# High and low parts of x^T side by side: one 512-column product with the high weights, and the halves added on eviction

## The chip, the cores and the metric

The kernel runs on one core of one Trainium2 chip. The metric is device time in microseconds from start to end of the program, the median of several runs. TensorE (PE) multiplies, VectorE (DVE) and ScalarE (ACT) read its results out of PSUM and prepare its operands, GpSimd (POOL) does a few small powers, and SyncE (SP) issues the DMAs that bring the weights.

## The reference

Four transformer blocks and then a fifth of another kind work on x of 256 tokens by 1024 features, all in fp32. The parts that the change touches, cut down:

```python
def conv_glu_ffn(x, w_up, conv_w, conv_b, w_down):      # four times, D_FF = 2816
    h = causal_depthwise_conv(x @ w_up, conv_w, conv_b) # kernel of 3 tokens
    g, u = jnp.split(h, 2, axis=-1)
    return (jax.nn.silu(g) * u) @ w_down
...
q = rope(q, cos, sin, dk); k = rope(k, cos, sin, dk)    # retention: 4 heads of 256, q and k from u @ w_in
...
f = jnp.square(jax.nn.relu(v2 @ w_up[i])) @ w_down[i]   # the fifth block's MLP, 4096 wide
```

Between them lie attention of several kinds, a linear recurrence, cross attention to a memory, and norms.

## The kernel before

An fp32 product is made of three products in TensorE's faster fp32r format: each operand is split into a high part (ScalarE, `split`, L200) and the low rest (VectorE, L201), and high x high, high x low and low x high are added up in PSUM. The activations stand transposed in two tiles, `xTh` and `xTl`, of 128 partitions x 8 chunks k x 256 tokens. `mm_T` (L218 to L225) makes the three products of one chunk for a result of 128 features x 256 tokens: the weights are the stationary operand, 256 token columns stream past them, and every product loads its weights anew (wh for L222 and L223, wl for L224). `proj_T` runs over the eight chunks, which is called a block of up products here. `mm_nat` (L214 to L216) is the other orientation, with 512 weight columns streaming.

Weights come in 512 KB pieces: a DMA into one of 5 `raw` tiles, then `split` into one of 9 pairs of `wh` and `wl` tiles of 1024 columns. A queue of each engine runs in program order, which a scheduler has fixed when the kernel was built; semaphores make one engine wait for another.

A feed-forward block (`ffn`, phases b0f to b3f) goes over 11 pairs p of 256 features. `up(p)` makes four blocks: for the gate half and the value half (b), two blocks (j), of which j = 0 lies in a PSUM bank of tag `sc` and j = 1 in one of tag `tr`, two banks of each tag. `conv` reads each block three times: ScalarE scales the last tap and adds the bias (L520), VectorE adds the two older taps (L522). `glu` then takes a tanh on ScalarE (L528), two steps on VectorE (L529, L530), and splits the result into `q` (high, ScalarE) and `pT` (low, VectorE). `down` of an earlier pair follows each `up`: 24 products of 512 columns into four banks that gather the block's result. The pairs 0 and 1 take their up products in the other orientation and are transposed (`nat_up`), which makes the start of a block rich in VectorE's work; the last pairs' down products come together in `down_end`. From pair 4 on, `up(p)` and a `down` make one period.

`mlp` does the same for 16 pairs without convolution: one bank holds both halves of a pair, VectorE takes maximum with 0 (L1443) and square (L1444). `ret_proj` projects q and k of a retention head into one bank of tag `sc` and rotates them on VectorE straight out of PSUM. The gates of the recurrence, the latent attention and the memory's keys use `proj_T` too.

Of the kernel before, what the change touches and what calls it, by code (L numbers as in the profile page):

```python
# [12 lines left out]
F32 = mybir.dt.float32  # L13
F32R = mybir.dt.float32r
I32 = mybir.dt.int32
AF = mybir.ActivationFunctionType
ALU = mybir.AluOpType
AX = mybir.AxisListType.X

P = 128  # L20
D = 1024
T = 256
NT = 2
KD = D // P
# [139 lines left out]
class Net:  # L164
# [66 lines left out]
    def proj_T(self, ps, cols, c0, Th, Tl):  # L231
        if Th is self.xTh:
            self.need()
        for k in range(cols.K):
            self.mm_T(ps, cols.get(k), slice(c0, c0 + P), Th[:, k, :], Tl[:, k, :], k == 0, k == cols.K - 1)

    def defer(self, cols, t, f):

        self.pend.append((self.work + cols, t, f))
# [36 lines left out]
            self.T_split(src, hi, lo)  # L276

    def new_xT(self):
        self.xTh = self.xp.tile([P, KD, T], F32R, tag="xTh", name=self.nm("xTh"))
        self.xTl = self.xp.tile([P, KD, T], F32R, tag="xTl", name=self.nm("xTl"))  # L280

    def new_oT(self):
        return (self.op.tile([P, KD, T], F32R, tag="oTh", name=self.nm("oTh")),
# [226 lines left out]
    def ffn(self, i, cc, pool):  # L510
        nc, I = self.nc, self.I
# [4 lines left out]
        def conv(ps, b, p):  # L516
            hc = self.s("e", [2, T])
            for j in range(2):
                f = b * NFT + 2 * p + j
                nc.scalar.activation(hc[:, j], ps[j], AF.Identity, bias=cc[:, 3, f : f + 1], scale=cc[:, 2, f : f + 1])  # L520
                for s in (1, 2):
                    nc.vector.scalar_tensor_tensor(hc[:, j, s:], ps[j][:, : T - s], cc[:, 2 - s, f : f + 1],  # L522
                                                   hc[:, j, s:], ALU.mult, ALU.add)
            return hc
# [10 lines left out]
        def up(p):  # L535
            gu = []
            for b in range(2):
                w = self.cols(W, b * DFF + p * 256, 256)
                pss = []
                for j in range(2):  # L540
                    ps = self.ps(("sc", "tr")[j], (T,))
                    self.proj_T(ps, w, j * P, self.xTh, self.xTl)
                    pss.append(ps)
                gu.append(conv(pss, b, p))
            return glu(*gu)

        def nat_up(nat, p):
# [31 lines left out]
        nat = self.op.tile([P, 2, 2, 512], F32, tag="oTh", name=self.nm("nat"))  # L579
        nat = [self.nat_chunk(ws, t, nat[:, t]) for t in range(NT)]  # L580
        hl[2] = up(2)
        hl[0] = nat_up(nat, 0)
        hl[3] = up(3)
        hl[1] = nat_up(nat, 1)
        tail = self.ln_tail(i, 2)
# [294 lines left out]
    def mla(self, j, mp):  # L880
        nc, I = self.nc, self.I
# [28 lines left out]
        sc = 192.0 ** -0.5  # L910
# [69 lines left out]
        down(1)  # L980
        norm(0)
        norm(1)
        v = self.xp.tile([P, 2, D], F32, tag="xTh", name=self.nm("v"))
        for hf in range(2):
            wq, wkv, qrT = w = weights(hf)
            for t in range(NT):
# [290 lines left out]
    def ret_proj(self, out, h):  # L1277
        nc = self.nc
        W = self.I["w_in_2"][0]
        for c0, tag in ((0, "C"), (1024, "D")):  # L1280
            w = self.cols(W, c0 + h * 256, 256)
            ps = self.ps("sc", (2, T))
            for j in range(2):
                self.proj_T(ps[:, j], w, j * P, self.xTh, self.xTl)
            a, b = self.b2(tag, [2, T]), self.s("e", [2, T])
            C = self.cos[:, None, :T].to_broadcast([P, 2, T])
            S = self.sin[:, :T]
            nc.vector.tensor_mul(a, ps, C)
            nc.vector.tensor_mul(b[:, 0], ps[:, 1], S)
            nc.vector.tensor_mul(b[:, 1], ps[:, 0], S)  # L1290
            nc.vector.tensor_sub(a[:, 0], a[:, 0], b[:, 0])
            nc.vector.tensor_add(a[:, 1], a[:, 1], b[:, 1])
            out.append(a)
            yield
        w = self.cols(W, 2048 + h * 512, 512)
        v, sg = self.b2("A", [2, 512]), self.b2("B", [2, 512])
        out += [v, sg]
        for t in range(NT):
            ps = self.ps("sc")
            self.proj_nat(ps, self.xTh, self.xTl, t, w)  # L1300
            nc.scalar.activation(v[:, t], ps, AF.Copy)
            yield
        w = self.cols(W, 4096 + h * 512, 512)
        for t in range(NT):
            ps = self.ps("sc")
            self.proj_nat(ps, self.xTh, self.xTl, t, w)
            a = sg[:, t]
            nc.scalar.activation(a, ps, AF.Tanh, scale=0.5)
            nc.vector.scalar_tensor_tensor(a, a, 1.0, ps, ALU.add, ALU.mult)
            yield  # L1310
# [120 lines left out]
    def mlp(self):  # L1431
        nc, I = self.nc, self.I
# [3 lines left out]

        def up(p):
            w = self.cols(W, p * 256, 256)
            ps = self.ps(("sc", "tr")[p % 2], (2, T))
            for j in range(2):  # L1440
                self.proj_T(ps[:, j], w, j * P, self.xTh, self.xTl)
            r, r2 = self.s("e", [2, T]), self.s("p", [2, T])
            nc.vector.tensor_scalar_max(r, ps, 0.0)  # L1443
            nc.vector.tensor_mul(r2, r, r)  # L1444
            hi, lo = self.s("q", [2, T], F32R), self.s("pT", [2, T], F32R)
            self.split(r2, hi, lo)
            return hi, lo
# [42 lines left out]
        for p in range(5, NPR):  # L1490
            hl[p] = up(p)
            flush(p - 1)
            if p == 7:
                e = self.ple_e()
# [126 lines left out]
```

## Time and profile before

| | |
|---|---|
| runs | 2077.45, 2081.17, 2081.6 us; median 2081.17 |
| profiled execution | 2078.6 us, span 2076.8 |
| TensorE busy | 2040.2 us, 98% of the span, 12213 products and as many weight loads |
| VectorE, ScalarE busy | 1539.4 us (74%), 1196.2 us (58%) |
| TensorE's clock | 2.4 GHz, mean granted share 0.997 |
| DMA | 359.83 MB, mean 173 GB/s |

Busy time of TensorE is modelled from its pipelined products, so starts of successive products tell more than durations. An engine's idle time matters only where TensorE ends up waiting for it.

### The profile page before, as it was taken

The numbers are of one execution on the slowest core, as the hardware profiler recorded it, in microseconds if no ns is written. First come the engines' busy times: TensorE is split into PE (matmuls) and PEld (weight loads), VectorE is DVE, ScalarE is ACT, GpSimd is POOL, SyncE is SP. The second block draws the span as 40 slices with busy tenths as digits, with TensorE's granted clock in tenths as the row PEclk, the third lists the DMA queues.
The fourth block names the chain that finished last, engine by engine and source line by source line (L and its number), as shares of the span: only waits on it lengthen the run. The fifth ranks groups of instructions, "written<-read, shape, count | busy, mean of one in ns | idle before, by whom it ended". The sixth has DMA issues, their size and how long they took to land.

```text
span 2076.8 us, 33251 instructions
## 1 busy us (share of the span) xinstructions
PE 2040.2 (98%) x12213; PEld 1784.0 (86%) x12213; DVE 1539.4 (74%) x2972; ACT 1196.2 (58%) x2408; POOL 39.8 (2%) x54
## 2 busy tenths in 40 slices
PE   7999999999999999999999999999999999999998
PEld 6878999887899988889997789998898888788896
DVE  7766887899697777779778778878666665676666
ACT  5844655596476546556656556555675444555544
POOL 0000000000000000000000000000000000000000
PEclk9999999999999999999999999999999999999999
DMA  7353666447466543565654436664545556566562
GB/s 269 127 187 115 210 209 188 147 134 249 137 202 194 171 161 111 183 198 179 190 156 160 144 124 213 215 187 120 164 123 192 166 176 203 166 199 206 188 188 76
DMA packets 236659, 359.83 MB, mean 173 GB/s; under 512 B 13904, under 2 KB 157392, under 8 KB 236496
## 3 DMA queue, kind: packets, MB, share of 16 engines
q1 hardware_dynamic: 236496, 357.71, 53.8%
q8 instruction: 96, 1.57, 0.3%
q14 instruction: 67, 0.55, 0.1%
HBM read 356.60 MB, written 1.05 MB: 172 GB/s over the span
## 4 chain that ended last, share of the span: by engine, by line
PE 52%; DVE 3%; ACT 2%; DMA 1%; issue 1%; POOL 0%; SPq 0%; POOLq 0%; DVEq 0%; ACTq 0%
PE mlp.acc L214 1%; PE mlp.acc L215 1%; PE mlp.acc L216 1%; PE b3f.tr L222 1%; PE b3f.sc L222 1%; PE b2f.tr L224 1%; PE b2f.tr L223 1%; PE b2f.tr L222 1%; PE b3f.tr L223 1%; PE b3f.tr L224 1%; PE b2f.sc L224 1%; PE b3f.sc L224 1%; PE b3f.sc L223 1%; PE b2f.sc L223 1%; PE b2f.sc L222 1%; PE b2f.acc L214 1%
## 5 line engine op out<-in xcount | busy, mean ns | idle before, releaser
L201 DVE TENSOR_TENSOR mlp.wl<-mlp.raw,mlp.wh 128x512 fp32r<-128x512 f32 x132 | 86.0, 687 | 56.1 <-ACT mlp.wh L200 55.2
L200 ACT ACTIVATE mlp.wh<-mlp.raw 128x512 fp32r<-128x512 f32 x132 | 75.8, 624 | 59.3 <-issue 23.5
L200 ACT ACTIVATE b0f.wh<-b0f.raw 128x512 fp32r<-128x512 f32 x132 | 77.4, 624 | 33.4 <-PE b0f.tr L223 11.9
L200 ACT ACTIVATE b1f.wh<-b1f.raw 128x512 fp32r<-128x512 f32 x132 | 77.4, 624 | 32.8 <-PE b1f.tr L223 11.9
L200 ACT ACTIVATE b2f.wh<-b2f.raw 128x512 fp32r<-128x512 f32 x132 | 77.5, 624 | 32.2 <-PE b2f.tr L223 11.9
L200 ACT ACTIVATE b3f.wh<-b3f.raw 128x512 fp32r<-128x512 f32 x132 | 77.3, 624 | 28.8 <-PE b3f.tr L223 10.3
L201 DVE TENSOR_TENSOR b0f.wl<-b0f.raw,b0f.wh 128x512 fp32r<-128x512 f32 x132 | 85.7, 686 | 9.2 <-ACT b0f.wh L200 7.2
L201 DVE TENSOR_TENSOR b1f.wl<-b1f.raw,b1f.wh 128x512 fp32r<-128x512 f32 x132 | 85.7, 686 | 8.4 <-ACT b1f.wh L200 6.4
L201 DVE TENSOR_TENSOR b2f.wl<-b2f.raw,b2f.wh 128x512 fp32r<-128x512 f32 x132 | 85.6, 686 | 8.0 <-ACT b2f.wh L200 6.1
L201 DVE TENSOR_TENSOR b3f.wl<-b3f.raw,b3f.wh 128x512 fp32r<-128x512 f32 x132 | 85.7, 686 | 7.4 <-ACT b3f.wh L200 5.4
L222 PE MATMUL b3f.tr<-b3xo.xTh,b3f.wh 128*128 128x256 f32 x144 | 40.8, 283 | 0.0
L222 PE MATMUL b0f.sc<-b0xo.xTh,b0f.wh 128*128 128x256 f32 x144 | 40.8, 283 | 0.0
L222 PE MATMUL b1f.sc<-b1xo.xTh,b1f.wh 128*128 128x256 f32 x144 | 40.8, 283 | 0.0
L222 PE MATMUL b2f.sc<-b2xo.xTh,b2f.wh 128*128 128x256 f32 x144 | 40.8, 283 | 0.0
L222 PE MATMUL b3f.sc<-b3xo.xTh,b3f.wh 128*128 128x256 f32 x144 | 40.8, 283 | 0.0
L224 PE MATMUL b0f.tr<-b0xo.xTh,b0f.wl 128*128 128x256 f32 x144 | 40.8, 283 | 0.0
L224 PE MATMUL b1f.tr<-b1xo.xTh,b1f.wl 128*128 128x256 f32 x144 | 40.8, 283 | 0.0
L224 PE MATMUL b2f.tr<-b2xo.xTh,b2f.wl 128*128 128x256 f32 x144 | 40.8, 283 | 0.0
L222 PE MATMUL b0f.tr<-b0xo.xTh,b0f.wh 128*128 128x256 f32 x144 | 40.8, 283 | 0.0
L223 PE MATMUL b0f.tr<-b0xo.xTl,b0f.wh 128*128 128x256 f32 x144 | 40.8, 283 | 0.0
L222 PE MATMUL b1f.tr<-b1xo.xTh,b1f.wh 128*128 128x256 f32 x144 | 40.8, 283 | 0.0
L223 PE MATMUL b1f.tr<-b1xo.xTl,b1f.wh 128*128 128x256 f32 x144 | 40.8, 283 | 0.0
(1636 smaller groups left out, 7630.2 us busy)
## 6 DMA issues: line engine op xcount, KB each, us to landing
b0f.raw<-in_f_w_up_dram SPq DMA_DIRECT2D x44, 512.0 KB
b1f.raw<-in_f_w_up_dram SPq DMA_DIRECT2D x44, 512.0 KB
b2f.raw<-in_f_w_up_dram SPq DMA_DIRECT2D x44, 512.0 KB
b3f.raw<-in_f_w_up_dram SPq DMA_DIRECT2D x44, 512.0 KB
mlp.raw<-in_w_up_dram SPq DMA_DIRECT2D x32, 512.0 KB
mlp.raw<-in_w_down_dram SPq DMA_DIRECT2D x32, 512.0 KB
b0f.raw<-in_f_w_down_dram SPq DMA_DIRECT2D x22, 512.0 KB
b1f.raw<-in_f_w_down_dram SPq DMA_DIRECT2D x22, 512.0 KB
```

The source lines that it names most:

```text
L200: self.nc.scalar.activation(hi, src, AF.Copy)
L201: self.nc.vector.tensor_sub(lo, src, hi.bitcast(F32))
L214: mm(ps, Th[:, k, tok(t)], wh, start=start, stop=False)
L215: mm(ps, Th[:, k, tok(t)], wl, start=False, stop=False)
L216: mm(ps, Tl[:, k, tok(t)], wh, start=False, stop=stop)
L222: mm(ps, wh[:, cs], rh, start=start, stop=False)
L223: mm(ps, wh[:, cs], rl, start=False, stop=False)
L224: mm(ps, wl[:, cs], rh, start=False, stop=stop)
```

## The change

`xTh` and `xTl` become the two halves of one tile `xT` of 8 chunks x 2 x 256 columns. A new function `proj_x` takes the place of `proj_T` in the feed-forward blocks, in `mlp` and for q and k of the retention; the other callers of `proj_T` keep it. Per chunk, the high weights meet both halves in one product of 512 columns that fills a whole bank: the first half of the bank gathers wh x xTh, the second wh x xTl. The low weights meet xTh in a product of 256 columns that is added into the second half. At the end ScalarE copies the second half to SBUF, and VectorE adds the first half to it. The convolution, the rotation and the square then read from SBUF instead of PSUM; in `mlp` maximum and square become one instruction, and a half of a pair takes a bank of its own. The tile `v` of the latent attention, which shared the place of `xTh`, is now declared as large as `xT`.

```diff
@@ -234,6 +234,29 @@
         for k in range(cols.K):
             self.mm_T(ps, cols.get(k), slice(c0, c0 + P), Th[:, k, :], Tl[:, k, :], k == 0, k == cols.K - 1)
 
+    def proj_x(self, dst, tag, w, c0):
+
+
+        self.need()
+        ps = self.ps(tag, (2, T))
+        mm = self.nc.tensor.matmul
+        cs = slice(c0, c0 + P)
+        for k in range(w.K):
+            wh, wl = w.get(k)
+
+            def high():
+                mm(ps.rearrange("p a n -> p (a n)"), wh[:, cs], self.xT[:, k].rearrange("p a n -> p (a n)"),
+                   start=k == 0, stop=k == w.K - 1)
+
+            def low():
+                mm(ps[:, 1], wl[:, cs], self.xTh[:, k], start=False, stop=False)
+
+            for f in (high, low) if k == 0 else (low, high):
+                f()
+            self.tick(T)
+        self.nc.scalar.activation(dst, ps[:, 1], AF.Copy)
+        self.nc.vector.tensor_add(dst, ps[:, 0], dst)
+
     def defer(self, cols, t, f):
 
         self.pend.append((self.work + cols, t, f))
@@ -276,8 +299,8 @@
             self.T_split(src, hi, lo)
 
     def new_xT(self):
-        self.xTh = self.xp.tile([P, KD, T], F32R, tag="xTh", name=self.nm("xTh"))
-        self.xTl = self.xp.tile([P, KD, T], F32R, tag="xTl", name=self.nm("xTl"))
+        self.xT = self.xp.tile([P, KD, 2, T], F32R, tag="xT", name=self.nm("xT"))
+        self.xTh, self.xTl = self.xT[:, :, 0], self.xT[:, :, 1]
 
     def new_oT(self):
         return (self.op.tile([P, KD, T], F32R, tag="oTh", name=self.nm("oTh")),
@@ -536,12 +559,10 @@
             gu = []
             for b in range(2):
                 w = self.cols(W, b * DFF + p * 256, 256)
-                pss = []
+                s = self.s("p", [2, T])
                 for j in range(2):
-                    ps = self.ps(("sc", "tr")[j], (T,))
-                    self.proj_T(ps, w, j * P, self.xTh, self.xTl)
-                    pss.append(ps)
-                gu.append(conv(pss, b, p))
+                    self.proj_x(s[:, j], ("sc", "tr")[j], w, j * P)
+                gu.append(conv([s[:, 0], s[:, 1]], b, p))
             return glu(*gu)
 
         def nat_up(nat, p):
@@ -980,7 +1001,7 @@
         down(1)
         norm(0)
         norm(1)
-        v = self.xp.tile([P, 2, D], F32, tag="xTh", name=self.nm("v"))
+        v = self.xp.tile([P, 2, 2, D], F32, tag="xT", name=self.nm("v"))[:, 0]
         for hf in range(2):
             wq, wkv, qrT = w = weights(hf)
             for t in range(NT):
@@ -1279,10 +1300,9 @@
         W = self.I["w_in_2"][0]
         for c0, tag in ((0, "C"), (1024, "D")):
             w = self.cols(W, c0 + h * 256, 256)
-            ps = self.ps("sc", (2, T))
+            a, b, ps = self.b2(tag, [2, T]), self.s("e", [2, T]), self.s("e", [2, T])
             for j in range(2):
-                self.proj_T(ps[:, j], w, j * P, self.xTh, self.xTl)
-            a, b = self.b2(tag, [2, T]), self.s("e", [2, T])
+                self.proj_x(ps[:, j], "sc", w, j * P)
             C = self.cos[:, None, :T].to_broadcast([P, 2, T])
             S = self.sin[:, :T]
             nc.vector.tensor_mul(a, ps, C)
@@ -1436,12 +1456,10 @@
 
         def up(p):
             w = self.cols(W, p * 256, 256)
-            ps = self.ps(("sc", "tr")[p % 2], (2, T))
+            r, r2 = self.s("e", [2, T]), self.s("p", [2, T])
             for j in range(2):
-                self.proj_T(ps[:, j], w, j * P, self.xTh, self.xTl)
-            r, r2 = self.s("e", [2, T]), self.s("p", [2, T])
-            nc.vector.tensor_scalar_max(r, ps, 0.0)
-            nc.vector.tensor_mul(r2, r, r)
+                self.proj_x(r[:, j], ("sc", "tr")[j], w, j * P)
+            nc.vector.scalar_tensor_tensor(r2, r, 0.0, r, ALU.max, ALU.mult)
             hi, lo = self.s("q", [2, T], F32R), self.s("pT", [2, T], F32R)
             self.split(r2, hi, lo)
             return hi, lo
```

TensorE's queue at the first block of up products in feed-forward block 1 (tile names carry a number; `b1xo.xTh`, `b1xo.xTl` and `b1xo.xT` hold the transposed activations), before:

```order
L222 MATMUL b1f.sc_5962<-b1xo.xTh_5680,b1f.wh_5965 128x256
L223 MATMUL b1f.sc_5962<-b1xo.xTl_5681,b1f.wh_5965 128x256
L224 MATMUL b1f.sc_5962<-b1xo.xTh_5680,b1f.wl_5966 128x256
L222 MATMUL b1f.sc_5962<-b1xo.xTh_5680,b1f.wh_5965 128x256
L223 MATMUL b1f.sc_5962<-b1xo.xTl_5681,b1f.wh_5965 128x256
L224 MATMUL b1f.sc_5962<-b1xo.xTh_5680,b1f.wl_5966 128x256
L222 MATMUL b1f.sc_5962<-b1xo.xTh_5680,b1f.wh_5965 128x256
```

The same place of TensorE's queue now:

```order
L248 MATMUL b1f.sc_5759<-b1xo.xT_5477,b1f.wh_5762 128x512
L252 MATMUL b1f.sc_5759<-b1xo.xT_5477,b1f.wl_5763 128x256 x2
L248 MATMUL b1f.sc_5759<-b1xo.xT_5477,b1f.wh_5762 128x512
L252 MATMUL b1f.sc_5759<-b1xo.xT_5477,b1f.wl_5763 128x256
L248 MATMUL b1f.sc_5759<-b1xo.xT_5477,b1f.wh_5762 128x512
L252 MATMUL b1f.sc_5759<-b1xo.xT_5477,b1f.wl_5763 128x256
```

Two products of each chunk's three are one, and from the second chunk on the low weights come first.

VectorE's queue in a steady period of the same block, from the first read of a pair's first block on (`e` is the convolution's tile, `p` the tanh's), before:

```order
L522 SCALAR_TENSOR_TENSOR b1f.e_6876<-b1f.sc_6810,b1x.cols_5208,b1f.e_6876 128x255
L522 SCALAR_TENSOR_TENSOR b1f.e_6876<-b1f.sc_6810,b1x.cols_5208,b1f.e_6876 128x254
L201 TENSOR_TENSOR b1f.wl_7101<-b1f.raw_7098,b1f.wh_7100 128x512 x2
L201 TENSOR_TENSOR b1f.wl_7161<-b1f.raw_7158,b1f.wh_7160 128x512
L522 SCALAR_TENSOR_TENSOR b1f.e_6876<-b1f.tr_6851,b1x.cols_5208,b1f.e_6876 128x255
L201 TENSOR_TENSOR b1f.wl_7161<-b1f.raw_7158,b1f.wh_7160 128x512
L522 SCALAR_TENSOR_TENSOR b1f.e_6876<-b1f.tr_6851,b1x.cols_5208,b1f.e_6876 128x254
L529 SCALAR_TENSOR_TENSOR b1f.e_6876<-b1f.p_6956,b1f.e_6876 128x512
L522 SCALAR_TENSOR_TENSOR b1f.e_6949<-b1f.sc_6883,b1x.cols_5208,b1f.e_6949 128x255
L522 SCALAR_TENSOR_TENSOR b1f.e_6949<-b1f.sc_6883,b1x.cols_5208,b1f.e_6949 128x254
```

The same place of VectorE's queue in a steady period now (`p` is also the tile of the added halves):

```order
L258 TENSOR_TENSOR b1f.p_6518<-b1f.sc_6519,b1f.p_6518 128x256
L545 SCALAR_TENSOR_TENSOR b1f.e_6573<-b1f.p_6518,b1x.cols_5005,b1f.e_6573 128x255
L545 SCALAR_TENSOR_TENSOR b1f.e_6573<-b1f.p_6518,b1x.cols_5005,b1f.e_6573 128x254
L201 TENSOR_TENSOR b1f.wl_6773<-b1f.raw_6770,b1f.wh_6772 128x512 x2
L258 TENSOR_TENSOR b1f.p_6518<-b1f.tr_6554,b1f.p_6518 128x256
L201 TENSOR_TENSOR b1f.wl_6825<-b1f.raw_6822,b1f.wh_6824 128x512 x2
L545 SCALAR_TENSOR_TENSOR b1f.e_6573<-b1f.p_6518,b1x.cols_5005,b1f.e_6573 128x255
L545 SCALAR_TENSOR_TENSOR b1f.e_6573<-b1f.p_6518,b1x.cols_5005,b1f.e_6573 128x254
L258 TENSOR_TENSOR b1f.p_6580<-b1f.sc_6581,b1f.p_6580 128x256
L552 SCALAR_TENSOR_TENSOR b1f.e_6573<-b1f.p_6642,b1f.e_6573 128x512
```

An add (L258) now stands ahead of each block's two convolution steps, and weight splits move by a place or two; their number in a period stays 12.

VectorE's queue at the start of that block, up to the low part `pT` of pair 0, before:

```order
L522 SCALAR_TENSOR_TENSOR b1f.e_6214<-b1f.sc_6148,b1x.cols_5208,b1f.e_6214 128x255
L529 SCALAR_TENSOR_TENSOR b1f.e_6121<-b1f.p_6140,b1f.e_6121 128x512
L522 SCALAR_TENSOR_TENSOR b1f.e_6133<-b1f.tr_6128,b1x.cols_5208,b1f.e_6133 128x255
L522 SCALAR_TENSOR_TENSOR b1f.e_6214<-b1f.sc_6148,b1x.cols_5208,b1f.e_6214 128x254
L522 SCALAR_TENSOR_TENSOR b1f.e_6133<-b1f.tr_6128,b1x.cols_5208,b1f.e_6133 128x254
L522 SCALAR_TENSOR_TENSOR b1f.e_6214<-b1f.tr_6189,b1x.cols_5208,b1f.e_6214 128x255
L530 SCALAR_TENSOR_TENSOR b1f.e_6133<-b1f.e_6121,b1f.e_6133 128x512
L522 SCALAR_TENSOR_TENSOR b1f.e_6214<-b1f.tr_6189,b1x.cols_5208,b1f.e_6214 128x254
L201 TENSOR_TENSOR b1f.wl_6426<-b1f.raw_6423,b1f.wh_6425 128x512
L201 TENSOR_TENSOR b1f.pT_6145<-b1f.e_6133,b1f.q_6144 128x512
```

The same place at the start of the block now, up to the same low part:

```order
L545 SCALAR_TENSOR_TENSOR b1f.e_5907<-b1f.tr_5902,b1x.cols_5005,b1f.e_5907 128x254
L552 SCALAR_TENSOR_TENSOR b1f.e_5895<-b1f.p_5914,b1f.e_5895 128x512
L258 TENSOR_TENSOR b1f.p_5922<-b1f.sc_5923,b1f.p_5922 128x256
L553 SCALAR_TENSOR_TENSOR b1f.e_5907<-b1f.e_5895,b1f.e_5907 128x512
L258 TENSOR_TENSOR b1f.p_5922<-b1f.tr_5958,b1f.p_5922 128x256
L545 SCALAR_TENSOR_TENSOR b1f.e_5977<-b1f.p_5922,b1x.cols_5005,b1f.e_5977 128x255
L258 TENSOR_TENSOR b1f.p_5984<-b1f.sc_5985,b1f.p_5984 128x256
L201 TENSOR_TENSOR b1f.pT_5919<-b1f.e_5907,b1f.q_5918 128x512
```

The adds of pair 3's first three blocks stand in front of this low part now, and three of the four convolution steps of pair 3 that stood there come behind it.

## Rows read from the trace of the kernel before

**Rows 1.** Page, busy time and instructions of each engine; TensorE's granted clock by slice.
```profile
PE 2040.2 (98%) x12213; PEld 1784.0 (86%) x12213; DVE 1539.4 (74%) x2972; ACT 1196.2 (58%) x2408; POOL 39.8 (2%) x54
...
PEclk9999999999999999999999999999999999999999
```

**Rows 2.** TensorE's longest wait: total us, times, longest us.
```profile
PE b0swa.acc L214 <- ACT start.xTh L200: 5.5, 2, 4.9
```

**Rows 3.** Groups by line, TensorE: count, then busy us, mean ns and idle us before.
```profile
L222 PE MATMUL b1f.sc<-b1xo.xTh,b1f.wh 128*128 128x256 f32 x144 | 40.8, 283 | 0.0
L222 PE MATMUL mlp.sc<-wo.xTh,mlp.wh 128*128 128x256 f32 x96 | 27.1, 283 | 0.0
L222 PE MATMUL rp1.sc<-b3f.xTh,rp1.wh 128*128 128x256 f32 x32 | 9.1, 285 | 0.0
```

**Rows 4.** Timeline, TensorE in feed-forward block 1: start us, duration us, line, operation.
```profile
699.97 0.28 PE L224 MATMUL b1f.tr<-b1xo.xTh,b1f.wl 128*128 128x256 f32 x1
707.17 0.28 PE L224 MATMUL b1f.tr<-b1xo.xTh,b1f.wl 128*128 128x256 f32 x1
707.29 0.40 PE L214 MATMUL b1f.acc<-b1f.wh,b1f.q 128*128 128x512 f32 x1
712.08 0.39 PE L214 MATMUL b1f.tq<-b1f.wh,b1f.q 128*128 128x512 f32 x1
```

**Rows 5.** Windows, two periods: us; PE, PEld, DVE, ACT, POOL busy; clock; DMA.
```profile
645.66:662.64 16.98, 16.98 (x122) 16.02 (x121) 13.13 (x23) 10.11 (x20) 0.00 (x0) 1.00 0.59 186
662.64:679.62 16.98, 16.98 (x122) 16.02 (x121) 13.13 (x23) 10.11 (x20) 0.00 (x0) 1.00 0.59 186
```

**Rows 6.** Groups by line, VectorE, 600 to 800 us: operands of 128x256.
```profile
L622 DVE TENSOR_TENSOR b2mla.e<-b2mla.acc,ropeC 128x256 f32<-128x256 f32 x4 | 1.7, 416 | 0.0
L626 DVE TENSOR_TENSOR b2mla.e<-b2mla.e,b2mla.e 128x256 f32<-128x256 f32 x4 | 1.7, 418 | 0.0
```

**Rows 7.** Groups by line, ScalarE, 600 to 800 us: operands of 128x256.
```profile
L200 ACT ACTIVATE b2mla.oTh<-b2mla.po 128x256 fp32r<-128x256 f32 x3 | 1.2, 384 | 4.2 <-PE b2mla.po L972 4.2
L200 ACT ACTIVATE b2mla.wh<-b2mla.raw 128x256 fp32r<-128x256 f32 x6 | 2.4, 406 | 0.0
```

**Rows 8.** Groups by line, ScalarE, three periods: idle us before them, releaser.
```profile
L200 ACT ACTIVATE b1f.wh<-b1f.raw 128x512 fp32r<-128x512 f32 x38 | 22.5, 625 | 6.1 <-PE b1f.tr L223 5.2 <-PE b1f.tq L216 0.8
L200 ACT ACTIVATE b1f.q<-b1f.e 128x512 fp32r<-128x512 f32 x3 | 1.9, 632 | 5.9 <-DVE b1f.e L530 5.9
L528 ACT ACTIVATE b1f.p<-b1f.e 128x512 f32<-128x512 f32 x3 | 1.9, 632 | 3.7 <-DVE b1f.e L522 3.7
```

**Rows 9.** Groups by line, VectorE, the same three periods.
```profile
L201 DVE TENSOR_TENSOR b1f.wl<-b1f.raw,b1f.wh 128x512 fp32r<-128x512 f32 x36 | 23.7, 687 | 2.2 <-ACT b1f.wh L200 1.2
L522 DVE SCALAR_TENSOR_TENSOR b1f.e<-b1f.sc,b1x.cols,b1f.e 128x255 f32<-128x255 f32 x6 | 2.9, 480 | 4.5 <-ACT b1f.e L520 4.5
L529 DVE SCALAR_TENSOR_TENSOR b1f.e<-b1f.p,b1f.e 128x512 f32<-128x512 f32 x3 | 2.1, 693 | 2.3 <-ACT b1f.p L528 2.3
L201 DVE TENSOR_TENSOR b1f.pT<-b1f.e,b1f.q 128x512 fp32r<-128x512 f32 x3 | 2.1, 693 | 2.3 <-ACT b1f.q L200 2.3
```

**Rows 10.** Start of feed-forward block 1: window as rows 5; then VectorE's and TensorE's timeline.
```profile
578.85:597.60 18.75, 18.75 (x159) 18.75 (x158) 17.05 (x35) 14.29 (x27) 0.00 (x0) 1.00 0.46 145
...
578.85 1.00 DVE L522 SCALAR_TENSOR_TENSOR b1f.e<-b1f.sc,b1x.cols,b1f.e 128x255 f32<-128x255 f32 x2 [0.59 <-ACT b1f.e L520]
596.91 0.69 DVE L201 TENSOR_TENSOR b1f.pT<-b1f.e,b1f.q 128x512 fp32r<-128x512 f32 x1
...
600.41 0.40 PE L216 MATMUL b1f.acc<-b1f.wh,b1f.pT 128*128 128x512 f32 x1
```

**Rows 11.** End of feed-forward block 1: timeline of VectorE, then TensorE.
```profile
728.25 0.69 DVE L201 TENSOR_TENSOR b1f.pT<-b1f.e,b1f.q 128x512 fp32r<-128x512 f32 x1 [0.76 <-ACT b1f.q L200]
...
730.19 0.39 PE L216 MATMUL b1f.acc<-b1f.wh,b1f.pT 128*128 128x512 f32 x1
```

**Rows 12.** Groups by line, VectorE, 1830 to 2000 us.
```profile
L1443 DVE TENSOR_SCALAR mlp.e<-mlp.sc 128x512 f32<-128x512 f32 x4 | 2.7, 684 | 0.0
```

## Prediction

> **What bounds the kernel now.** I read the page's busy times first: of a span of 2076.8 us TensorE is busy 2040.2, at the full clock in every slice [rows 1], so all its waits together are 36.6 us. The longest of them, by the view of who waits for whom, stands at the kernel's first stage [rows 2]. The groups by line then show that the products this change touches wait for nothing: idle 0.0 us before them in the feed-forward blocks, in `mlp` and in the retention projections [rows 3]. So time is won or lost in two ways only: by how long TensorE's stream of products is, and by whether the other engines still keep ahead of it.
>
> The timeline gives the stream's price. From one 256-column product at 699.97 us to another at 707.17 lie 60 steps: 0.1200 us each. From 707.29 to 712.08 lie 21 steps of 512 columns: 0.2281 us each [rows 4]. (The durations in such rows, 0.28 and 0.40, overlap; the starts count.) Twice the columns cost less than twice the time: each product carries about 0.012 us that doesn't depend on its width. The boundary between the kinds shows no price of its own: the first wide product starts 0.12 us after the last narrow one [rows 4].
>
> **The change, part by part.** *Removed on TensorE.* Per weight chunk k, three products of 256 columns (0.360 us) become one of 512 and one of 256. A feed-forward block in its steady state repeats a period of 16.98 us, all of it TensorE's [rows 5]: 4 blocks of 24 narrow products and 24 wide ones of the down projection. 96 x 0.120 = 11.52 leaves 5.46 for 24 wide ones, 0.2275 each, boundaries included. So a merge saves 0.240 - 0.2275 = 0.0125 us by the period, 0.0119 by the steps. The merged products are counted by the L222 groups: 8 groups of 144 in four feed-forward blocks, 2 of 96 in `mlp`, 4 of 32 in retention [rows 3]: 1152 + 192 + 128 = 1472. That is 17.5 to 18.4 us; I take 18.2. 1472 weight loads go too; they lay beside the products and give nothing more.
>
> The Trainium skill speaks against this size: in "TensorE: Matmul & The Clock Gate", section Back-to-back issue gap, the gap of a warm product is its columns over 2.4 plus 2.5 ns, which makes 109 and 216 ns where the rows have 120 and 228. By that rule a merge would save 2.5 ns and the whole change 3.7 us.
>
> *Added on eviction.* One ScalarE copy and one VectorE add of 128x256 for each of 184 blocks (36 in each feed-forward block, 24 in `mlp`, 16 in retention). The trace has no such add of the kernel's own, but rope's products of the same shape took 416 ns from PSUM and 418 from SBUF [rows 6], so I take 0.418, and where a source moves from PSUM to SBUF (the convolution, the rotation) VectorE gains and loses nothing. A ScalarE eviction of 128x256 took 384 ns from PSUM, a conversion of that size from SBUF 406 [rows 7]: 0.384 for the copy, and some 0.02 more for each convolution start that now reads SBUF.
>
> *Feed-forward, steady state.* VectorE 13.13 + 4 x 0.418 = 14.80 us and ScalarE 10.11 + 4 x 0.41 = 11.75 us [rows 5], in a period that shrinks by 32 x 0.0125 to 16.58. Both fit, if their waits give way: VectorE has 3.85 us of idle per period and may keep 1.78. Over three periods its idle is 4.5 us before the convolution's first step (which hangs on TensorE ending a block), 2.2 before weight splits, and 2.3 + 2.3 behind ScalarE's tanh and high part [rows 9]. Only the last two hang on VectorE's own chain: 1.53 us a period, under 1.78 by a quarter of a microsecond. ScalarE's conversions wait for TensorE to free a weight buffer [rows 8], nine of which hold one and a half periods (6 buffers are used up in one), so a late VectorE eats that lead before TensorE stands. I price the steady state at no loss.
>
> *Feed-forward, start.* Here VectorE is full: of the 18.75 us from 578.85 to the end of the low part at 597.60 it is busy 17.05, and TensorE reads that low part at 600.41 [rows 10]. The order ahead of it gains 7 adds and loses 3 convolution steps that now come later, 7 x 0.418 - 3 x 0.48 = 1.5 us; TensorE, two groups of up products nearer, arrives 0.8 us earlier. 2.8 - 1.5 - 0.8 leaves 0.5 us, more if the 1.7 us of idle fill. If nothing fills and an add in front of a full queue waits on TensorE as well, TensorE stands for about 1 us. Four such starts: 0 to 4 us, I take 0.6.
>
> *Feed-forward, end.* The last pair's low part is done at 728.94 and read at 730.19 [rows 11]: 1.25 us of room. Copy and add lengthen the chain from the last block by 0.384 + 0.418 and two handovers, about 0.9. Covered, by 0.3 us; without the cover up to 0.9 each at four ends. I take 0.4 in all.
>
> *`mlp` and retention.* In `mlp` maximum and square (0.684 us for the first [rows 12]) become one instruction, so VectorE pays 2 x 0.418 - 0.68 = 0.15 us per pair; the result is used one pair of up products later, over 5 us. Each half takes a bank of its own now, two of each tag, so a bank comes back after two pairs instead of four, still over 10 us. In retention two banks serve four halves: a bank's eviction has the other half's 2.78 us, against 0.8 for copy and add and up to two queued weight splits of 0.69 [rows 9]. The queued conversion or split in front of the copy is the work that could be late; I price it at nothing, 1 us at most over four heads.
>
> *Waits added.* ScalarE's convolution start now waits for VectorE's add, and behind it stand weight conversions; who waits for these is TensorE, one and a half periods later. Taking wl before wh at k > 0 asks for the low weights 0.24 us earlier, which that lead covers. DMAs stay the same in number and order.
>
> Sum: -18.2 + 0.6 + 0.4 = -17.2 us on the profiled execution's 2078.6 (span 2076.8, 1.8 around it): 2061.4. That execution lies 2.6 us under the median of the runs, 2081.17; from the median it would be 2063.9. I predict between them, 2062.5.
>
> **The rivals.** *A, VectorE's lag at the start of the feed-forward blocks reaches TensorE.* For it: the full stretch [rows 10], in which eight adds (3.3 us) fall. Against: PSUM is read out by two short steps instead of three, so banks come free earlier. If each of four blocks loses 2 us, with the ends 0.9: 11.6 of 18.2 come back, 2072; at half of it 2067.
>
> *B, the width-independent 0.012 us is mostly not saved*, because a product pays again when its neighbour has another width, which mixed runs now have all along. The rows show two pure runs and one boundary at 0.12, which speaks against it. With 0.0025 us left per merge: 1472 x 0.0025 = 3.7 us, 2075 to 2077. That is also the result of the skill's gap rule named above; the trace's 0.1200 and 0.2281 don't agree with it.
>
> *C, slower: ScalarE and VectorE hand each other the blocks and can't fill their idle.* The place is the steady period. Each add waits for a copy, each convolution start for an add, in queues that run in order. If VectorE's idle stays above 2.18 us a period (16.98 - 14.80), the period is longer than now; if all 3.85 stays it is 18.65, or 1.67 more in 28 periods, 47 us, less 4 us saved elsewhere: 2122. Against it: of the 3.85 only 1.53 is tied to VectorE's chain [rows 9].
>
> *D, more than the sum*, where TensorE's remaining 36.6 us of waits shrink as well; nothing in the profile asks for it: under 2058.
>
> **How the numbers follow.** The forecast (14 to 20 us off) 0.70, A 0.14, B 0.06, C 0.06, D 0.04. The range reaches from 2058, all of 18.4 and a low run, to 2072, rival A in full: it leaves out B, C and D, 0.16. A measurement of this kernel tells about 0.2%, 4.2 us, from no change: the forecast, A and D are faster by more than that, 0.88; B is within it, 0.06; C slower, 0.06.
>
> **What would show it.** In the changed profile 10741 products, 1472 of the merged form about 0.228 us apart from the next and 1472 narrow ones at 0.120; a period of 16.58 us with VectorE near 14.8 and ScalarE near 11.8 busy, and no idle before the up products. Adds near 0.42, copies near 0.38. A: idle before the first down products of each block, behind its low part. B: a pair of starts 0.357 apart instead of 0.347. C: periods over 16.98 with TensorE idle behind weight splits. I'm wrong if TensorE's total of waits grows by more than 5 us or if the pair isn't at 0.347.

## The result and the profile after

The changed kernel took 2067.65 us (median of 4 runs, 2066.98 to 2068.26), the kernel before 2080.75 (4 runs, 2077.45 to 2081.6): ratio 0.9934, 95% interval 0.9922 to 0.9946. Two later series of the changed kernel, 5 runs each, gave 2067.89 and 2069.42. 2062.5 was forecast, with 2058 to 2072 as the range: the time lies inside, 5 us above the centre. The profiled execution took 2067.32 us, 11.3 less than that of before, where the sum was 17.2.

The page's busy times of the engines:

```profile
PE 2027.3 (98%) x10741; PEld 1704.8 (83%) x10741; DVE 1587.2 (77%) x3144; ACT 1247.6 (60%) x2592; POOL 39.8 (2%) x54
```

Two of TensorE's waits, from the view of who waits for whom (total us, times, longest):

```profile
PE b0swa.acc L214 <- ACT start.xT L200: 5.1, 2, 4.5
...
PE b3f.sc L248 <- DVE b3f.e L545: 1.0, 1, 1.0
```

Against [rows 1]: 1472 products fewer, TensorE 12.9 us less busy, and its waits 2065.5 - 2027.3 = 38.2 us instead of 36.6. [rows 2] has come down by 0.4, and of the waits in the stages that the change touches one of 1.0 us is new (and one of 0.3 in `mlp`). So the other engines kept ahead, and what is missing in these stages is missing in the stream itself. Three steady periods of feed-forward block 1 in the windows (columns as in rows 5), with their sum, answer to [rows 5]:

```profile
643.38:660.00 16.62, 16.62 (x89) 14.25 (x88) 15.23 (x30) 10.89 (x22) 0.00 (x0) 1.00 0.67 212
660.00:676.63 16.63, 16.63 (x89) 14.25 (x88) 14.77 (x29) 11.73 (x24) 0.00 (x0) 1.00 0.66 198
676.63:693.26 16.63, 16.63 (x90) 14.25 (x88) 14.16 (x28) 11.10 (x23) 0.00 (x0) 1.00 0.63 192
sum 49.88, PE 49.88 PEld 42.75 DVE 44.16 ACT 33.71 POOL 0.00; mean PE 16.63 PEld 14.25 DVE 14.72 ACT 11.24 POOL 0.00
```

16.63 us, all of it TensorE's, where 16.98 stood and 16.58 was forecast: 0.35 us for 32 merges, 0.0109 each. TensorE's timeline inside the second of these periods shows why it isn't 0.0125:

```profile
660.82 0.40 PE L248 MATMUL b1f.sc<-b1xo.xT,b1f.wh 128*128 128x512 f32 x1
...
662.59 0.40 PE L248 MATMUL b1f.sc<-b1xo.xT,b1f.wh 128*128 128x512 f32 x1
662.82 0.40 PE L248 MATMUL b1f.tr<-b1xo.xT,b1f.wh 128*128 128x512 f32 x1
...
663.63 0.39 PE L248 MATMUL b1f.tr<-b1xo.xT,b1f.wh 128*128 128x512 f32 x1
...
665.36 0.40 PE L248 MATMUL b1f.tr<-b1xo.xT,b1f.wh 128*128 128x512 f32 x1
665.59 0.39 PE L248 MATMUL b1f.sc<-b1xo.xT,b1f.wh 128*128 128x512 f32 x1
```

From 660.82 to 662.59 lie five pairs of a wide and a narrow product: 0.354 us each. In the next block, from 663.63 to 665.36, five pairs take 0.346 each. The first block runs from 660.00 to 662.82, the second to 665.59: 2.82 and 2.77. Long and short blocks take turns like this from pair 4 of every feed-forward block on, and in `mlp`. Both are the same instructions on the same shapes at the full clock; I call the two patterns of starts the long and the short one. The groups by line show the same split as mean durations (count, then busy us, mean ns and idle us before), against [rows 3]:

```profile
L248 PE MATMUL b1f.sc<-b1xo.xT,b1f.wh 128*128 128x512 f32 x144 | 52.4, 398 | 0.0
...
L248 PE MATMUL b1f.tr<-b1xo.xT,b1f.wh 128*128 128x512 f32 x144 | 51.7, 394 | 0.0
```

The second missing piece is the clock. Windows over the stretches of the profiled execution in which TensorE's granted clock (the last but two of the columns) was at half, 1.2 GHz, ahead of the kernel's tail:

```profile
52.61:56.02 3.41, 3.41 (x14) 2.92 (x14) 2.60 (x5) 3.21 (x12) 0.00 (x0) 0.50 0.05 15
465.62:469.03 3.41, 3.41 (x9) 2.66 (x9) 3.41 (x6) 2.82 (x6) 0.00 (x0) 0.50 0.60 196
1435.01:1438.42 3.41, 3.40 (x13) 3.31 (x14) 2.06 (x7) 1.69 (x3) 0.00 (x0) 0.50 0.39 115
1462.31:1465.72 3.41, 3.41 (x15) 3.30 (x14) 1.16 (x5) 2.80 (x8) 0.00 (x0) 0.50 0.40 115
```

Four, and in the execution of before two (at 1212.7 and 1468.7 us). Each costs at most half its length, 1.7 us. The profiled difference then adds up: 1472 x 0.0109 = 16.0 saved, less 1.6 of waits and up to 3.4 of half clock, leaves 11.0 or more, where 11.3 was measured.

The stages themselves say it more directly. The windows over the four feed-forward blocks, the stages with q and k of the four retention heads, and `mlp`, each from its first product to the next stage's, have these sums, before and now:

```profile
sum 1018.49, PE 1017.83 PEld 932.80 DVE 776.37 ACT 589.20 POOL 10.78; mean PE 127.23 PEld 116.60 DVE 97.05 ACT 73.65 POOL 1.35
...
sum 1003.45, PE 1001.73 PEld 850.92 DVE 823.08 ACT 637.95 POOL 10.81; mean PE 125.22 PEld 106.36 DVE 102.89 ACT 79.74 POOL 1.35
```

The stages of the change are 15.0 us shorter, and the rest of the span, where all the stretches at half clock lie, is 3.7 us longer.

### The profile page after: what moved, and what is told of

Read it like the earlier page. It is cut to its first block, busy times and chain, and to the rows that moved or that the text cites. A ratio compares the mean times of both kernels' runs of the same rounds, so it can differ in the third digit from the quotient of the medians.

```text
span 2065.5 us, 30420 instructions
## 1 busy us (share of the span) xinstructions
PE 2027.3 (98%) x10741; PEld 1704.8 (83%) x10741; DVE 1587.2 (77%) x3144; ACT 1247.6 (60%) x2592; POOL 39.8 (2%) x54
## 4 chain that ended last, share of the span: by engine, by line
PE 51%; DVE 3%; ACT 2%; issue 1%; DMA 1%; POOL 0%; SPq 0%; POOLq 0%; DVEq 0%; ACTq 0%
PE b2f.sc L248 2%; PE b2f.tr L248 2%; PE b3f.sc L248 1%; PE b3f.tr L248 1%; PE mlp.sc L248 1%; PE mlp.tr L248 1%; PE mlp.acc L214 1%; PE mlp.acc L216 1%; PE mlp.acc L215 1%; PE b2f.acc L216 1%; PE b2f.sc L252 1%; PE b3f.acc L214 1%; PE b2f.acc L214 1%; PE b3f.acc L216 1%; PE b3f.acc L215 1%; PE b2f.acc L215 1%
## 5 line engine op out<-in xcount | busy, mean ns | idle before, releaser
L248 PE MATMUL b3f.sc<-b3xo.xT,b3f.wh 128*128 128x512 f32 x144 | 52.4, 398 | 1.0 <-DVE b3f.e L545 1.0
L248 PE MATMUL b1f.sc<-b1xo.xT,b1f.wh 128*128 128x512 f32 x144 | 52.4, 398 | 0.0
L248 PE MATMUL b2f.sc<-b2xo.xT,b2f.wh 128*128 128x512 f32 x144 | 52.4, 398 | 0.0
L248 PE MATMUL b0f.sc<-b0xo.xT,b0f.wh 128*128 128x512 f32 x144 | 52.4, 398 | 0.0
L248 PE MATMUL b2f.tr<-b2xo.xT,b2f.wh 128*128 128x512 f32 x144 | 51.8, 395 | 0.0
L248 PE MATMUL b0f.tr<-b0xo.xT,b0f.wh 128*128 128x512 f32 x144 | 51.7, 394 | 0.0
L248 PE MATMUL b1f.tr<-b1xo.xT,b1f.wh 128*128 128x512 f32 x144 | 51.7, 394 | 0.0
L248 PE MATMUL b3f.tr<-b3xo.xT,b3f.wh 128*128 128x512 f32 x144 | 51.7, 394 | 0.0
L545 DVE SCALAR_TENSOR_TENSOR b1f.e<-b1f.p,b1x.cols,b1f.e 128x255 f32<-128x255 f32 (+1 forms) x72 | 34.2, 479 | 6.8 <-ACT b1f.e L543 6.3
L545 DVE SCALAR_TENSOR_TENSOR b2f.e<-b2f.p,b2x.cols,b2f.e 128x255 f32<-128x255 f32 (+1 forms) x72 | 34.2, 478 | 6.8 <-ACT b2f.e L543 6.4
```

What stands on the lines that cost most here:

```text
L248: mm(ps.rearrange("p a n -> p (a n)"), wh[:, cs], self.xT[:, k].rearrange("p a n -> p (a n)"), start=k == 0, stop=k == w.K - 1)
```

## The experiments

**The merge undone, the eviction kept.** At the first chunk the wide product stays (it opens both halves of the bank at once), at the other seven it is split again.

```diff
-            for f in (high, low) if k == 0 else (low, high):
+            def narrow():
+                mm(ps[:, 0], wh[:, cs], self.xTh[:, k], start=False, stop=False)
+                mm(ps[:, 1], wh[:, cs], self.xTl[:, k], start=False, stop=k == w.K - 1)
+
+            for f in (high, low) if k == 0 else (low, narrow):
```

> The merge alone is undone: at seven of eight chunks three products of 256 columns again; banks of two halves, copy and add stay. If the eviction is nearly free and the products give the time, 1288 products come back at 0.360 - 0.349 = 0.0106 us, 13.7 us: 2081 us, and blocks of up products last 2.87 us. If the eviction costs several microseconds, this kernel must lie above the kernel before by that cost less the 2 us of the merges that stay: 2080.75 + 4 - 2 = 2083 us or more, with TensorE's waits longer than the 38.2 us now.

2082.47 us (11 runs) against 2081.26 of before (16 runs), ratio 1.0005 [0.9996, 1.0014]. A steady period in the windows:

```profile
666.29:683.23 16.94, 16.94 (x117) 15.81 (x116) 14.32 (x28) 11.24 (x23) 0.00 (x0) 1.00 0.63 192
```

16.94 where 28 unmerged products at 0.0109 ask for 16.63 + 0.31: the gain sits in the merge alone, and copy and add cost nothing in the steady state. With the 2.0 us (184 x 0.0109) of merges that stay, the median puts the eviction at 2082.47 + 2.0 - 2081.26 = 3.2 us for the whole kernel, give or take 2 by the interval, which decides between neither of the two expectations; TensorE's waits are 39.4 us here. By the sum over the stages (1020.5 us) it is 4.0. But 2.6 of that are waits for banks at the starts of the feed-forward blocks (0.32 in three, 1.59 in the last) where the changed kernel has one of 1.0, so this kernel shows more than the eviction costs there.

**The eviction undone, the merge kept** (feed-forward blocks; cut: the switch in `proj_x` that returns the bank's first half and leaves out copy and add).

```diff
-                s = self.s("p", [2, T])
-                for j in range(2):
-                    self.proj_x(s[:, j], ("sc", "tr")[j], w, j * P)
-                gu.append(conv([s[:, 0], s[:, 1]], b, p))
+                gu.append(conv([self.proj_x(None, ("sc", "tr")[j], w, j * P, False) for j in range(2)], b, p))
```

> In the feed-forward blocks copy and add are left out, and the convolution reads the first half of the bank; the second half (both small terms of the product) is left out of the result there. The products stay. If the eviction is hidden but for the one wait of 1.0 us in the last feed-forward block and some tenths at the others, 1 to 2 us less: 2066. If the eviction is what the missing 4 us of the forecast went to, 2063.5 or less, by waits that vanish at the starts of the blocks.

2065.48 us (5 runs, 2059.95 to 2067.79), ratio 0.9918 [0.9906, 0.993]: 2.2 under the changed kernel's first median. The period is 16.63 here too; the wait of 1.0 us in the last feed-forward block is down to 0.15, and the span differs by 1.8 us, of which one stretch at half clock less (three instead of four) explains up to 1.7. The sum over the stages, which no such stretch touches, is 1002.0 instead of 1003.45: 1.5 us, 0.9 of it in the last feed-forward block. So the eviction in these blocks costs one to two microseconds, mostly at that one place:

```profile
1277.50 0.47 PE L248 MATMUL b3f.sc<-b3xo.xT,b3f.wh 128*128 128x512 f32 x1 [1.02 <-DVE b3f.e L545]
```

In the changed kernel TensorE waits here for a bank of tag `sc` that the transposed pair 0 holds, until VectorE, full at the start of a block, gets to the convolution steps that read it.

**What makes a block long or short: high first in every chunk** (cut: the flag that ends a sum moves to the low product).

```diff
-            for f in (high, low) if k == 0 else (low, high):
+            for f in (high, low):
```

> High product before low product in every chunk, so that two of one width never follow each other. 84 blocks of up products last 2.776 us now and 83 last 2.814. Theory P (the two lengths are two patterns of one stream, and the pattern flips where two products of a kind follow each other): all blocks get one length, and the time is 3.2 us less (2064.5) or 3.2 us more (2070.9). Theory W (the length hangs on the bank or on which half of the weight columns is used): 2.78 and 2.81 alternate as now, 2067.6 us. Theory B (each change of width costs something): 16 changes instead of 14 inside and between blocks, about 0.006 us a block or 1 us more.

**Products of a kind in twos throughout.**

```diff
-            for f in (high, low) if k == 0 else (low, high):
+            for f in (low, high) if k % 2 else (high, low):
```

> High, low in even chunks and low, high in odd ones: products of one width come in twos, half as many changes of width. Theory P: the pattern is set anew all along, every block has one length; by the starts around the present twos (0.232 from a wide product on, 0.115 from a narrow one) 2.776 us, so 3.1 us less, 2064.5. Theory W: 2.78 and 2.81 still alternate, 2067.6 us. Theory B (each change of width costs 3 ns): 7 changes fewer in each of 184 blocks, 3.9 us less, and all blocks near 2.77.

2075.67 us (6 runs) and 2067.41 (5 runs); against before 0.9973 [0.9961, 0.9984] and 0.9931 [0.9918, 0.9945]. One steady period of `high_first`, then one of `by_twos`:

```profile
663.24:680.03 16.79, 16.79 (x89) 14.30 (x88) 14.33 (x28) 11.23 (x23) 0.00 (x0) 1.00 0.65 194
```

```profile
659.39:675.98 16.59, 16.59 (x89) 14.23 (x88) 14.29 (x28) 11.44 (x24) 0.00 (x0) 1.00 0.65 196
```

The order of two products in a chunk moves the time by 8 us, with the same instructions. With nothing of a kind in succession the stream, once in the long pattern, stays in it: all 28 blocks of the steady periods of block 1 last 2.81 to 2.83 us, on both tags, so theory W (bank or weight columns) is out. In the short pattern it stays too: two successive blocks of `high_first` in the retention's second head, then two in its third (windows as above):

```profile
1615.01:1620.56 5.55, 5.55 (x35) 4.89 (x34) 4.17 (x8) 2.97 (x6) 0.00 (x0) 1.00 0.56 172
1663.93:1669.59 5.66, 5.66 (x35) 4.91 (x33) 4.22 (x8) 2.96 (x6) 0.00 (x0) 1.00 0.51 172
```

2.77 and 2.83 a block, in one execution, with the same order and in banks of one tag: what differs is the pattern that the stream came in with. In twos every steady block lasts 2.78 to 2.79. Theory B, a price for each change of width, fits `by_twos`, but two changes more in a block can't make `high_first` 8 us slower, and it can't make blocks of equal order differ by 0.04 us. Theory P was right in kind and not in size. For `high_first` 3.2 us more were expected and 8 came. All of it lies in the stages of the change (1011.7 us instead of 1003.45): 4.5 in the 28 steady periods, 16.79 instead of 16.63; the rest, at the starts of the feed-forward blocks and in `mlp`, wasn't followed up. `by_twos` was to gain 3.1 us and gained 0.2 in the median; its stages are 1.7 us shorter (1001.8), and five stretches at half clock stand in its profile.

**A test of P by an order that it picks.** Each group high, low, low, high turned the pattern over. So a second such group in every block should leave all blocks of a length, the short one by the expectation.

```diff
-            for f in (high, low) if k == 0 else (low, high):
+            for f in (high, low) if k in (0, 2) else (low, high):
```

> High, low in chunks 0 and 2, low, high in the others: two places where products of one kind follow each other inside a block instead of one. Theory P says that each such HLLH group flips the stream between the long pattern (pairs of 0.3535 us) and the short one (0.346), so two of them in a block leave every block short behind its fourth chunk: about 2.776 us for all of them, 84 blocks by 0.038 less than now, 3.1 us: 2064.5. If the pattern is set only by what stands at a block's start or end, 2.78 and 2.81 alternate as now: 2067.6. If the order by twos is as good as it gets, 2.787 and 2066.

2066.82 us (5 runs), and its period:

```profile
660.27:676.83 16.56, 16.56 (x89) 14.21 (x88) 14.69 (x29) 11.70 (x24) 0.00 (x0) 1.00 0.67 203
```

Long and short blocks no longer take turns: all steady blocks last 2.775 to 2.78. The exception fits P better than its own expectation does. In the retention's second head, then in its third, two successive blocks of `flip_twice` last

```profile
1608.64:1614.28 5.64, 5.64 (x33) 4.90 (x32) 4.16 (x9) 2.96 (x6) 0.00 (x0) 1.00 0.53 161
1657.66:1663.22 5.56, 5.56 (x33) 4.86 (x32) 4.12 (x9) 2.97 (x6) 0.00 (x0) 1.00 0.54 163
```

2.82 and 2.78 each. By P two groups turn the pattern over twice, so a block hands on the pattern that it got, and the steady blocks are short because they got the short one. The period gives (16.98 - 16.56) / 32 = 0.0131 us per merge, a little over what the forecast took. The time had moved less than the blocks, so both kernels ran again:

> The same kernel as flip_twice, to see whether what its blocks lose arrives in the time: its up products took 2.75 us less than those of the changed kernel by their stages, but its median was only 0.8 to 1.1 us lower, with more stretches at half clock in its profile. If those stretches are chance, the median over both calls lies 2 to 3 us under that of the changed kernel, 2065; if the denser stream itself brings them, it stays within 1 us, 2066.8.

> The changed kernel once more, on the same chip as flip_twice_2: 2067.7 us, with the blocks of up products at 2.78 and 2.81 in turn.

2065.49 and 2069.42 us. All runs together: 2065.74 (10 runs, 2064.68 to 2067.5) against 2067.93 for the changed kernel (14 runs, 2065.02 to 2071.48), 2.2 us less, about what the shorter blocks promise (0.07 us in each of 28 steady periods is 2.0). The two ranges overlap; the sums over the stages, 1000.9 us in both profiles against 1003.45, say the same without the half clock. This is the fastest kernel of the study that computes the whole result: 0.9929 of before, interval 0.9916 to 0.9941, in the second series.

**How much VectorE can take.** VectorE makes the copies too.

```diff
-        self.nc.scalar.activation(dst, ps[:, 1], AF.Copy)
+        self.nc.vector.tensor_copy(dst, ps[:, 1])
```

> VectorE makes the copy of the second half too, four more steps of some 0.38 us per period: 14.72 + 1.5 = 16.2 us of a period of 16.63. If VectorE's idle gives way (the forecast's view), the steady period stays 16.63, and only the four starts suffer, where seven copies more stand in front of the first low part, 2.3 us against 1.6 us of room now, and where the banks of the transposed pairs come back later: 1 to 3 us each, 2071 to 2079 in all. If VectorE keeps its present idle of 1.9 us a period (rival C), the period becomes 18.1 us and 28 of them add 41 us: 2109.

2084.77 us (12 runs), 1.0016 [1.0007, 1.0024] of before: the whole gain is spent. The time lies beyond the 2071 to 2079 of the one theory and far under the 2109 of the other. Windows: one period, and the surroundings of a wait at the end of block 1:

```profile
667.81:684.44 16.63, 16.63 (x90) 14.25 (x88) 14.77 (x30) 9.22 (x17) 0.00 (x0) 1.00 0.70 216
...
734.40:738.52 4.12, 0.08 (x1) 0.00 (x0) 3.40 (x9) 1.22 (x3) 0.00 (x0) 1.00 0.43 99
738.52:741.93 3.41, 3.32 (x8) 2.60 (x9) 1.05 (x2) 0.04 (x1) 0.00 (x0) 0.50 0.27 92
```

The one VectorE group with idle ahead of it in three periods (busy us, mean ns, then idle and its releaser):

```profile
L545 DVE SCALAR_TENSOR_TENSOR b1f.e<-b1f.p,b1x.cols,b1f.e 128x255 f32<-128x255 f32 x10 | 4.8, 480 | 5.2 <-ACT b1f.e L543 5.2
```

TensorE's new waits:

```profile
PE b1f.acc L214 <- ACT b1f.q L200: 4.1, 1, 4.1
...
PE b2f.acc L214 <- ACT b2f.q L200: 3.7, 1, 3.7
PE b0f.acc L214 <- ACT b0f.q L200: 3.6, 1, 3.6
...
PE b3f.acc L214 <- ACT b3f.q L200: 2.0, 1, 2.0
```

The period is 16.63 to the hundredth: TensorE notices nothing in the steady state. But VectorE's only idle is now 5.2 us in three periods, all of it behind ScalarE's start of the convolution, a hand-over that it didn't fill; in the two periods after these it is busy 16.63 and 16.46 us. It falls behind: its adds start 1.0 us behind the end of their block on TensorE at the earliest in pair 4, 7.4 at the latest in pair 8 and 5.2 to 6.0 in the last pair, where the changed kernel has 0.6 to 1.1 in its last four pairs. The bill comes at the end of each block, where TensorE stands 2.0 to 4.1 us for the last pair's high part. I had expected it at the start. In block 1 the clock falls to half as the wait of 4.1 us ends, as the two windows at 734.40 and 738.52 show; it falls at the end of blocks 0 and 2 too. The profiled execution is 20.9 us longer than the changed kernel's (2086.4 against 2065.5): the four waits make 13.4 of it, and 30.7 us at half clock ahead of the tail instead of 13.7 can explain the rest.

**Where the clock falls.** The kernel before again, for a second profile (one run), and the changed one (5 runs).

> The kernel before, unchanged, for the places at which its clock falls. Its first profile has two stretches at half clock ahead of the last one, at 1212.7 and 1468.7 us. If the change brings the additional ones, at 53 us in the first stage and at 466 us in the second block's projections, they are missing here again. If they come and go with the execution, some of them are here, and the span is 1 to 2 us longer for each than 2076.8.

> The changed kernel, unchanged, beside the two above on one chip: 2067.6 us. If the stretches at half clock belong to the kernel, they stand at 53, 466, 1435 and 1462 us again; if they come and go, one or two are missing and the span is 1 to 2 us shorter for each.

2080.51 and 2067.89 us. Windows over two half-clock stretches of `before_again`, and over the projections behind the recurrence of block 1 (b1mo); after them the same stage in the first profile of before:

```profile
52.04:55.45 3.41, 3.41 (x12) 2.66 (x13) 1.79 (x3) 3.40 (x12) 0.00 (x0) 0.50 0.04 14
468.46:471.87 3.41, 3.41 (x9) 2.63 (x9) 3.41 (x7) 2.60 (x5) 0.00 (x0) 0.50 0.49 156
...
460.57:488.82 28.25, 25.57 (x104) 19.86 (x104) 25.37 (x45) 20.77 (x35) 0.92 (x1) 0.94 0.53 186
```

```profile
458.85:486.02 27.17, 24.27 (x104) 18.64 (x104) 25.29 (x45) 20.79 (x35) 0.92 (x1) 1.00 0.55 194
```

The unchanged kernel has the stretches at 52 and 468 us in one execution and not in the other, and the stage is 1.1 us longer with one. `after_again` lacks the one at 1435, and its span is 2063.2 instead of 2065.5 us. So these stretches come and go with the execution, and the first two don't need the change. That the change makes none more frequent is not shown: those two stand in all ten profiles of the changed kernel and its variants, and the one at 1435 in neither profile of before. The mean granted clock over the runs of each kernel is 0.9952 (14 of the changed one) and 0.9962 (42 of before), a difference worth 2 us at most.

The sums over the stages of the change don't depend on them. In the second profile of before, then in those of the two later series of the changed kernel:

```profile
sum 1018.39, PE 1017.73 PEld 932.84 DVE 775.67 ACT 589.50 POOL 10.82; mean PE 127.22 PEld 116.60 DVE 96.96 ACT 73.69 POOL 1.35
...
sum 1003.50, PE 1001.78 PEld 850.81 DVE 823.29 ACT 638.21 POOL 10.82; mean PE 125.22 PEld 106.35 DVE 102.91 ACT 79.78 POOL 1.35
...
sum 1003.38, PE 1001.67 PEld 850.84 DVE 823.21 ACT 637.84 POOL 10.80; mean PE 125.21 PEld 106.36 DVE 102.90 ACT 79.73 POOL 1.35
```

14.9 to 15.1 us less in every pair of executions, while the rest of the span takes 1058.3 and 1060.3 us before and 1059.7 to 1066.3 with the change. The stretches stand at few places, in or shortly behind a wait of TensorE, here in the changed kernel's timeline ahead of the first two listed above:

```profile
51.55 0.63 PE L279 MATMUL b0swa.tq<-ident,b0swa.e 128*128 128x128 f32 x4 [1.59 <-DMA b0swa.e<-in_mem_dram]
...
463.84 0.50 PE L214 MATMUL b1mo.acc<-b1mo.wh,b1lru.oTh 128*128 128x512 f32 x1 [1.87 <-ACT b1mo.wh L200]
465.14 0.47 PE L214 MATMUL b1mo.tq<-b1mo.wh,b1lru.oTh 128*128 128x512 f32 x1 [0.56 <-DVE b1lru.e L877]
```

The execution of before on which the sum was made had the fewest of all those profiled here, and lay 2.6 us under its median.

## Why the prediction held, and where it was off

**Removed on TensorE: right in kind, 13% too large.** The term was 18.2 us, 1472 merges at 0.0119 to 0.0125; it measured 1472 x 0.0109 = 16.0. The step that failed is the one from two pure runs and one boundary [rows 4] to a mixed stream. The pair was to be 0.347; it is 0.354 in every second block and 0.346 in the others. My own mark for being wrong, a pair that isn't at 0.347, is met in half of the blocks. `flip_twice`, whose steady blocks are all short, gives the forecast's size back. What in TensorE makes one pattern and the other was not found: the runs show which orders turn one into the other, no more.

**Rival B** had the place and not the size: a mixed stream does pay, but 0.0016 us per merge rather than 0.010. The Trainium skill ("TensorE: Matmul & The Clock Gate", section Back-to-back issue gap) would leave an estimated 2.5 ns per merge, by a formula that the section gives for a single isolated product and sets apart from a stream in which every product loads its weights, as here. The trace has 10.9 to 13.1 ns, so the measurement decides against its use for this kernel.

**Eviction, steady state: no loss, as forecast; the load's agreement is partly luck.** Copies took 376 to 377 ns and adds 417 to 420. VectorE was busy 14.72 us a period (14.80 forecast), but that is a mean of 15.23, 14.77 and 14.16 while it works off the start of the block; settled it is 14.16, so four adds raise its load by 1.03 us, not 1.67, in part because their durations overlap the next step's. ScalarE was busy 11.10 then (11.75 forecast). Rival C, at the load that the change brings, did not occur; `vector_copy` shows that it was not far. Four more VectorE steps per period are enough, and the price then is a wait at each block's end rather than a longer period.

**Feed-forward start and end: 0.6 + 0.4 forecast, one to two measured, at another place.** Against 16.0 us for the merges the stages of the change are 15.0 shorter, which leaves 1.0, and `first_half` says 1.5; that the size came out is luck, since the forecast had it elsewhere. The low part that rival A looked at had more room than I gave it. VectorE's and TensorE's timelines:

```profile
597.04 0.42 DVE L258 TENSOR_TENSOR b1f.p<-b1f.sc,b1f.p 128x256 f32<-128x256 f32 x1
597.37 0.68 DVE L201 TENSOR_TENSOR b1f.pT<-b1f.e,b1f.q 128x512 fp32r<-128x512 f32 x1
...
599.67 0.39 PE L216 MATMUL b1f.acc<-b1f.wh,b1f.pT 128*128 128x512 f32 x1
```

Done at 598.05 and read at 599.67: 1.6 us of room, 0.5 were forecast; the other three blocks have 1.6 as well. TensorE came 0.74 us earlier than in [rows 10], near the forecast's 0.8, and the low part only 0.45 later, where 1.5 less the idle that fills was forecast. (0.10 of the shift is that the block starts earlier.) One reason stands in the first two rows: an add that takes 0.42 is followed 0.33 later, so in a full queue it costs 0.33. The 1.0 us that VectorE's lag did cost came by a way that I had argued against ("banks come free earlier"): a bank of the transposed pairs, which are still read by three steps, comes back later; that the adds in VectorE's queue delay it fits `first_half`, where that wait is 0.15 us without them. At the ends TensorE waits for nothing in block 1.

**Waits added, `mlp`, retention:** nothing there worth a microsecond; TensorE's waits grew by 1.6 us, under the 5 that would have made me wrong.

**Not in the sum: the clock.** The prediction read "the full clock in every slice" from [rows 1], but a 9 there means 90% or more, and two stretches at half clock lie in that trace. That of the changed kernel had four, up to 3.4 us of the 5.9 that the profiled difference falls short of the sum. By stages, 2.2 of the 5.9 is missing in those that the change touches (17.2 against 15.0), and that is the merge's 18.2 against 16.0; the rest lies outside of them. Between the medians (13.1 us) the clock weighs less, since other runs of before have lower mean clocks too (0.995 to 0.998).

**The forecast and the range.** The time lies where rival A at half strength was priced, 2067, but A's cause makes only about 1.0 us of it, the wait in the last feed-forward block; the range held the time through its room for A, not because it foresaw the long pattern or the clock. (From the median the sum gives 2064.0, not 2063.9.)

## What to carry to other kernels

A product's price in a pure run is only a first estimate of its price in a mixed stream: after such a merge, read the starts block by block, and try the order of the products inside a chunk, which moved this kernel by 10 us at the same work. Where stretches at half clock come and go, compare the changed stages alone: here they gave 14.9 to 15.1 us in every pair of executions, while the spans gave anything from 7.1 to 15.5. When an engine off the path takes on work, ask which of its idle hangs on a hand-over: here that part wasn't filled, and the lag showed at the end of the stage, not in its period.

## What the runs showed of the hardware

- The same alternation of 512- and 256-column products, each with its own weights, runs in one of two lasting patterns, 0.346 or 0.354 us a pair; a group high, low, low, high turned the one into the other, and without such groups the stream stayed in the one it came in with: the long one for the steady part of every feed-forward block (blocks of 2.81 to 2.83 us), the short one for a retention head (2.77).
- Stretches of 3.41 to 10.24 us at half clock began in or within 4 us behind waits of 1.0 to 4.1 us of TensorE, in some executions and not in others of the same kernel, and one cost 1.1 us in the stage where the same kernel shows it with and without.
- In a full queue VectorE's next step started 0.33 us after a start of a 128x256 step whose duration is 0.42.
